# Twelve of 22 inner tiles of two feed-forwards go through the down projection in seven products of halves

## The chip, the cores and the metric

One Trainium2 chip; the kernel uses one of its cores. The metric is the device time of one execution in microseconds (us), measured on the chip. TensorE does the matmuls, VectorE and ScalarE the elementwise work, GpSimd some more of it, and SyncE (SP) issues the transfers between DRAM and the on-chip memory.

## What is computed

Two layers of a transformer trunk over 512 latent tokens and 256 context tokens with 1024 features. Each layer has a feed-forward, a mixer and a second feed-forward, all in float32:

```python
D_MODEL = 1024; SEQ = 512; CTX_LEN = 256; D_FF = 2816
def swiglu(h, w_gu, w_down):
    gu = h @ w_gu
    return (jax.nn.silu(gu[..., :D_FF]) * gu[..., D_FF:]) @ w_down
...
x = x + 0.5 * gt * swiglu(h, p["ffn1_w_gu"], p["ffn1_w_down"])
xc = xc + 0.5 * gtc * swiglu(hc, p["ffn1_w_gu"], p["ffn1_w_down"])
```

`h` is the normalized input, scaled and shifted by vectors of its own for latent and for context tokens; `gt` and `gtc` are gates, one per feature. All these vectors come from a projection of the conditioning (`w_mod`), nine of 1024 features per layer.

## The kernel before

Everything is kept transposed: 128 features on the partitions, 768 tokens in the free dimension, context first. The residual `xs` stays in four on-chip slots `xp` (two feature tiles each); `xd` is a DRAM tensor of the same shape, in which the mixers park the residual. Each float32 matrix is split into an upper part (rounded to TensorE's float32 format, by ScalarE) and a lower part (what is left, by VectorE); a product is the sum of three matmuls, upper-upper, upper-lower and lower-upper. `split` (L125 to L128) does it, for weights as for activations; `load_split` loads and splits a weight.

The stages run in the order first feed-forward, attention pair, second feed-forward, third feed-forward, linear attention, fourth feed-forward. A feed-forward (`ffn`) goes over the inner dimension in 22 tiles of 128. They are grouped in `PARTS` of 6, 6, 5 and 5 tiles. For each tile, gate and up are computed, multiplied and split into `hid[f]` (six buffers). After each part its tiles go through the down projection: for each quarter u of the output (two feature tiles of 128) the weights are loaded, `pair` issues the matmuls for 256 context and 512 latent columns, and `add_gated` (L398) adds the gated result to the residual. The last part goes through `close_out`, which also prepares the next stage's input.

From tile 4 on (5 in the last feed-forward), gate and up are computed by `seven_open`'s `unit`: the matrix [gate; up] times [first half | second half of the tokens] is a 2x2 block product, which is done in seven block products in place of eight (Strassen's method in Winograd's form). The sums of the activations (T1 to T4) are made once per feed-forward, those of the weights (S1 to S4) in each unit, and the sums of the products behind the matmuls, on VectorE and ScalarE. One product is 12 matmuls with 384 columns. The `product` helper accumulates in one bank of a ring of eight.

The conditioning's projection is background work of VectorE: `mod_step` takes steps from a queue, each of which loads 256 KB and does two multiply-and-sum instructions of 512 columns (L297), one for each of the two conditioning vectors. `bg` says how many steps follow each unit and each quarter; `mod_step(1000)` does the rest.

Instructions are written in program order; a scheduler with a model of the engines orders them for each engine before the run. Buffers are rings of fixed size: `raw` three, `whi` and `wlo` three, `sg` one.

Of the kernel before, what the change touches and what calls it, by code (L numbers as in the profile page):

```python
# [21 lines left out]
CTX = 256  # L22
# [3 lines left out]
PARTS = [(0, 6), (6, 6), (12, 5), (17, 5)]  # L26
EPS = 1e-6
# [20 lines left out]
class Net:  # L48
# [54 lines left out]
    def load_split(self, src, n, pool=None, keep=4, slots=(None, None)):  # L103
# [3 lines left out]
        for j in range(2):  # L107
            raw = self.raw(src[:, j * (n // 2):(j + 1) * (n // 2)])
# [10 lines left out]
    def raw(self, src):  # L119
        n = src.shape[-1]  # L120
        raw = self.stage.tile([128, 1024], F32, tag="raw", name="raw", bufs=3)[:, :n]
        self.nc.sync.dma_start(out=raw, in_=src)
        return raw

# [47 lines left out]
    def mod_finish(self, l, p):  # L172
# [4 lines left out]
        for v in range(2):  # L177
# [4 lines left out]
        if p % 3 == 2 and p != 5:  # L182
            nc.vector.tensor_scalar(out=m, in0=m, scalar1=0.5, scalar2=None, op0=ALU.mult)

# [93 lines left out]
    def mod_step(self, n):  # L278
        nc = self.nc
        self.owed += n  # L280
        while self.owed >= 1 and self.pending:
            self.owed -= 1
            l, p, m, i = self.pending.pop(0)
            if i == 0 and m == 0 and p == 0:
                nc.sync.dma_start(out=self.bmod[l], in_=self.ins[f"b_mod{l}"])
                nc.sync.dma_start(out=self.ng[l], in_=self.ins[f"norm_g{l}"])
# [7 lines left out]
            for v in range(2):  # L294
# [4 lines left out]
            if i and m == KT - 1:  # L299
                nc.vector.tensor_tensor(out=self.mod[l][p], in0=self.mod[l][p], in1=self.acc, op=ALU.add)  # L300
                self.mod_finish(l, p)
# [150 lines left out]
    def ffn(self, l, sub, idx, segs, nxt, bg=(0, 0), first=4, start=False):  # L452
# [12 lines left out]
        st = ExitStack()  # L465
        with st:
# [6 lines left out]

            def up(f, ss, regs=None):
# [4 lines left out]
                if f not in hid:  # L479
                    hidden(f)  # L480
                sg = pool.tile([128, T], F32, tag="sg", name="sg", bufs=1)
# [4 lines left out]
                self.split(sg[:, a:b], hid[f][0][:, a:b], hid[f][1][:, a:b])  # L486
# [32 lines left out]
            for pi, (f0, nf) in enumerate(PARTS):  # L519
                for f in range(f0, f0 + nf):  # L520
                    if f >= early:
                        if f >= first:
                            if f == first:
                                sp = seven_start()
                                if self.pending:
                                    self.mod_open(self.pool("modp", sts, side="right"))
                            hidden(f)
                            sg = pool.tile([128, T], F32, tag="sg", name="sg", bufs=1)
                            seven(sp, gu[f], sg, hid[f])
# [6 lines left out]
                dn = self.ins[f"dn{l}{idx}_{nf}"][pi % 2 if nf == 6 else pi - 2]  # L536
                load = lambda u: self.load_split(dn[u], 2 * nf * 128)
                if pi == len(PARTS) - 1:
# [3 lines left out]
                    h = self.close_out(load, nf, xk, segs, gate, nxt)  # L542
                else:
                    for u in range(4):
# [4 lines left out]
                        self.mod_step(bg[1])  # L549
        yield h  # L550

    def seven_open(self, st, h, n0):
# [7 lines left out]
        sub = lambda o, a, b: nc.vector.tensor_tensor(out=o, in0=a, in1=b, op=ALU.subtract)  # L560

# [26 lines left out]
        def weights(a):  # L588
            hi = self.stage.tile([128, 1024], F32R, tag="whi", name="whi", bufs=3)
            lo = self.stage.tile([128, 1024], F32R, tag="wlo", name="wlo", bufs=3)  # L590
            res = []
            for i, x in enumerate(a):
                c = slice(i * 512, (i + 1) * 512)
                self.split(x(), hi[:, c], lo[:, c])
                res.append((hi[:, c], lo[:, c]))
            return res

        def product(o, w, x, first, last):
            for k in range(H):
                y = [a[:, k * 128:(k + 1) * 128] for a in w]  # L600
                for i, (wi, xi) in enumerate(((0, 0), (0, 1), (1, 0))):
                    nc.tensor.matmul(out=o, lhsT=y[wi], rhs=x[k][xi], start=first and k == 0 and i == 0,  # L602
# [1228 lines left out]
```

## Time and profile before

| what | value |
|---|---|
| time, median of 3 runs | 2709.84 us (2709.37 to 2710.6) |
| time of the profiled execution | 2708.46 us |
| its span, first to last instruction | 2706.7 us |
| mean granted clock of TensorE | 0.99 of full speed |
| TensorE busy | 2617.1 us (97%) |
| VectorE busy | 2161.1 us (80%) |
| ScalarE busy | 1196.9 us (44%) |
| GpSimd busy | 171.6 us (6%) |

The profile shows one execution; outside its span lie 1.8 us. Busy times are unions of the instructions' times. Those of matmuls overlap in the records, so the pace of matmuls is read from stretches divided by counts, not from the mean of one. Idle time of an engine that is not the bottleneck costs nothing.

### The profile page before, as it was taken

The page shows a single profiled execution, that of the slowest core. Times are in us where ns is not written, and L with a number is a line of the kernel's source. Part 1 is how long each engine was busy: PE and PEld are TensorE (multiplying, and loading weights), DVE is VectorE, ACT ScalarE, POOL GpSimd, SP SyncE. Part 2 cuts the span into 40 slices and gives each one's busy share as a digit, 9 for nine tenths or more (in the row PEclk, how much of TensorE's full clock was granted, in tenths as well). Part 3 has the DMA queues.
Part 4 walks back from the last instruction along what each step waited for, and adds up shares of the span by engine and source line. Part 5 has one row for each costly group of instructions (what it writes and reads, how often), then busy time and mean ns, then how long its engine had stood idle before and what let it go on. Part 6 is the DMA issues. An engine that isn't in the chain of part 4 may idle for free. (4 is left out here: it accounts for less than half of the span.)

```text
span 2706.7 us, 44030 instructions
## 1 busy us (share of the span) xinstructions
PE 2617.1 (97%) x16800; PEld 2435.1 (90%) x16800; DVE 2161.1 (80%) x4503; ACT 1196.9 (44%) x2254; POOL 171.6 (6%) x206
## 2 busy tenths in 40 slices
PE   7999999999878899999999999999999999999999
PEld 5899999989777789899999999999998998989899
DVE  6789798977888867797988878888777677778677
ACT  4324242445757744242424542424345565435344
POOL 0000000013443200000000000000000121000000
PEclk9999999999989999999999999999999999999999
DMA  8143444431000140433343314343232121422334
GB/s 313 42 150 115 139 132 145 124 126 42 24 24 1 47 141 30 129 114 127 117 141 100 115 63 138 108 145 104 92 116 86 56 71 63 148 71 92 102 106 128
DMA packets 103572, 279.31 MB, mean 103 GB/s; under 512 B 12256, under 2 KB 15200, under 8 KB 101824
## 3 DMA queue, kind: packets, MB, share of 16 engines
q1 hardware_dynamic: 103360, 276.50, 31.4%
q8 instruction: 132, 2.16, 0.3%
q14 instruction: 80, 0.66, 0.1%
HBM read 269.11 MB, written 7.34 MB: 102 GB/s over the span
## 5 line engine op out<-in xcount | busy, mean ns | idle before, releaser
L127 ACT ACTIVATE whi<-raw 128x512 fp32r<-128x512 f32 (+3 forms) x466 | 355.7, 767 | 739.9 <-PE r L374 326.4
L128 DVE TENSOR_TENSOR wlo<-raw,whi 128x512 fp32r<-128x512 f32 (+3 forms) x466 | 399.2, 859 | 81.0 <-ACT whi L127 78.2
L602 PE MATMUL r<-t,whi 128*128 128x384 f32 (+1 forms) x1704 | 400.9, 323 | 1.8 <-DVE u L639 1.3
L602 PE MATMUL r<-hh,wlo 128*128 128x384 f32 (+1 forms) x1136 | 366.1, 323 | 0.0
L602 PE MATMUL r<-hh,whi 128*128 128x384 f32 (+1 forms) x1136 | 365.8, 322 | 0.0
L602 PE MATMUL r<-hl,whi 128*128 128x384 f32 (+1 forms) x1136 | 365.7, 322 | 0.0
L297 DVE SCALAR_TENSOR_TENSOR junk<-wm,cb 128x512 bf16<-128x512 f32 x480 | 329.1, 686 | 13.4 <-ACT cb L276 8.3
L602 PEld LDWEIGHTS r<-t,whi 128*128 128x128 f32 x1704 | 295.6, 188 | 3.2 <-DVE u L639 2.1
L602 PE MATMUL r<-t,wlo 128*128 128x384 f32 (+1 forms) x852 | 273.3, 323 | 0.0
L374 PE MATMUL r<-dh,whi 128*128 128x512 f32 (+1 forms) x952 | 267.3, 345 | 0.8 <-ACT whi L127 0.8
L374 PE MATMUL r<-dh,wlo 128*128 128x512 f32 (+1 forms) x952 | 266.8, 346 | 0.3 <-DVE wlo L128 0.3
L374 PE MATMUL r<-dl,whi 128*128 128x512 f32 (+1 forms) x952 | 266.8, 344 | 0.0
L127 ACT ACTIVATE whi<-s 128x512 fp32r<-128x512 f32 x284 | 174.6, 625 | 182.4 <-DVE s L624 67.0
L602 PEld LDWEIGHTS r<-hl,whi 128*128 128x128 f32 x1136 | 213.4, 188 | 0.8
L602 PEld LDWEIGHTS r<-hh,wlo 128*128 128x128 f32 x1136 | 213.4, 188 | 0.4 <-DVE wlo L128 0.4
L602 PEld LDWEIGHTS r<-hh,whi 128*128 128x128 f32 x1136 | 213.3, 188 | 0.3
L374 PEld LDWEIGHTS r<-dh,wlo 128*128 128x128 f32 x952 | 178.6, 188 | 24.4 <-DVE wlo L128 1.1
L374 PEld LDWEIGHTS r<-dh,whi 128*128 128x128 f32 x952 | 178.0, 188 | 24.5 <-ACT whi L127 2.7
L374 PEld LDWEIGHTS r<-dl,whi 128*128 128x128 f32 x952 | 178.1, 188 | 23.5
L128 DVE TENSOR_TENSOR wlo<-s,whi 128x512 fp32r<-128x512 f32 x284 | 190.7, 684 | 4.4 <-ACT whi L127 3.7
L398 DVE SCALAR_TENSOR_TENSOR x<-r,mod,x 128x512 f32<-128x512 f32 (+1 forms) x168 | 100.1, 632 | 90.8 <-PE r L374 90.3
L602 PEld LDWEIGHTS r<-t,wlo 128*128 128x128 f32 x852 | 159.9, 188 | 0.1
(417 smaller groups left out, 5845.1 us busy)
## 6 DMA issues: line engine op xcount, KB each, us to landing
raw<-gu SPq DMA_DIRECT2D x176, 512.0 KB, 3.9
wm<-w_mod SPq DMA_DIRECT2D x240, 256.0 KB, 2.9
raw<-dn SPq DMA_DIRECT2D x88, 320.0 KB, 2.9
raw<-dn SPq DMA_DIRECT2D x64, 384.0 KB, 3.1
raw<-w_out SPq DMA_DIRECT2D x28, 512.0 KB, 3.8
m<-w_mod0a SPq DMA_DIRECT2D x12, 1024.0 KB, 10.4
raw<-w_in SPq DMA_DIRECT2D x8, 512.0 KB, 4.8
raw<-w_kq SPq DMA_DIRECT2D x8, 512.0 KB, 3.7
```

What stands on the lines that cost most here:

```text
L127: self.nc.scalar.activation(out=hi, in_=src, func=AF.Copy)
L128: (e or self.nc.vector).tensor_tensor(out=lo, in0=src, in1=hi.bitcast(F32), op=ALU.subtract)
L297: nc.vector.scalar_tensor_tensor(out=junk, in0=w, scalar=1.0, in1=self.cb[:, v, :], op0=ALU.mult, op1=ALU.mult, accum_out=self.acc[:, m, v ...
L374: nc.tensor.matmul(out=outs[s][j], lhsT=w[j][wi][:, k * 128:(k + 1) * 128], rhs=xk[k][xi][:, s0:s1], start=(k == 0 and i == 0), stop=(k == ...
L398: self.nc.vector.scalar_tensor_tensor(out=self.xs[m][:, s0:s1], in0=regs[s][j], scalar=gate[:, m, v:v + 1], in1=self.xs[m][:, s0:s1], op0= ...
L602: nc.tensor.matmul(out=o, lhsT=y[wi], rhs=x[k][xi], start=first and k == 0 and i == 0, stop=last and k == H - 1 and i == 2, skip_group_che ...
```

## The change

In the second and third feed-forward the parts become (0, 4), (4, 4), (8, 4), (12, 4) and (16, 6); the three in the middle are marked `by7`. For these, the down projection of four inner tiles and one quarter of the output is a 2x2 block product too: output tiles j = 0, 1, pairs of inner tiles, halves of the tokens (384 columns). It is done in seven products of 2 x 3 matmuls. The results are not summed on chip: ScalarE multiplies each (or a partial sum that accumulates in a bank) by the gate and writes it to a buffer, and GpSimd sends the buffer with an accumulating DMA to `xd`. Before the first such part the residual is written to `xd`; after the last it is read back. Its on-chip slots serve meanwhile as buffers: sums of the hidden tiles, and halves to send.

`finished` makes the sums of the hidden tiles. `unit` is rewritten for all four feed-forwards: weights are split in pieces of 1024 columns, three banks serve in place of four, one accumulates four products and is copied out in between, and a few VectorE operations fall away. In `mod_step` the last four vectors of the second layer are made for one conditioning vector only, and the steps are shared out anew. The weights of a part whose tiles lie in two stored groups are loaded in several pieces.

```diff
+PLAIN = [(f0, n, False) for f0, n in PARTS]
+SEVEN = [(0, 4, False), (4, 4, True), (8, 4, True), (12, 4, True), (16, 6, False)]
...
+    def mod_vectors(self, l, p):
+        return 1 if l == 1 and p >= 5 else 2
...
-            self.owed -= 1
             l, p, m, i = self.pending.pop(0)
+            nv = self.mod_vectors(l, p)
+            self.owed -= nv / 2
...
+            def finished(f, sg):
+                if f not in place:
+                    if f not in hid:
+                        hidden(f)
+                    self.split(sg[:, n0:T], *[x[:, n0:T] for x in hid[f]])
+                    return
+                q = place[f]
+                hidden(f)
+                if q < 2:
+                    sub(sg[:, hi], sg[:, hi], sg[:, lo])
+                    self.split(sg[:, n0:T], *[x[:, n0:T] for x in hid[f]])
+                    return
+                o = self.kept[:, q - 2, :]
+                self.split(sg[:, n0:T], *[x[:, n0:T] for x in hid[f]])
+                sub(o[:, hi], sg[:, hi], o[:, hi])
+                sub(o[:, lo], o[:, hi], o[:, lo])
+                sub(sg[:, lo], sg[:, lo], o[:, hi])
+                hidden(f + 100)
+                self.split(o[:, n0:T], *[x[:, n0:T] for x in hid[f + 100]])
+                self.split(sg[:, lo], *[self.t4[:, i, (q - 2) * n:(q - 1) * n] for i in range(2)])
...
+            def down_seven(sp, f0, u, buf, late):
...
+                raw = self.raw(sum([self.down_weights(l, idx, f0, 4, u, j) for j in range(2)], []))
+                A11, A12, A21, A22 = [raw[:, i:i + 256] for i in range(0, 1024, 256)]
...
+                self.split(raw[:, 0:512], *[x[:, 0:512] for x in w1])
+                nc.vector.tensor_tensor(out=S1, in0=A21, in1=A22, op=ALU.add)
+                sub(S2, S1, A11)
+                self.split(s[:, 0:512], *[x[:, 512:1024] for x in w1])
+                sub(A21, A11, A21)
+                self.split(raw[:, 512:1024], *[x[:, 0:512] for x in w2])
+                sub(A12, A12, S2)
+                self.split(A12, *cut(w2, 2))
...
+                def out(o, x, j, s):
+                    c = sorted({s.start, s.stop, min(max(CTX, s.start), s.stop)})
+                    for a, b in zip(c, c[1:]):
+                        nc.scalar.activation(out=o[:, a - s.start:b - s.start], in_=x[:, a - s.start:b - s.start],
+                                             func=AF.Copy, scale=gate[:, 2 * u + j, int(a < CTX):int(a < CTX) + 1])
+                def send(o, j, s):
+                    d = self.xd[:, 2 * u:2 * u + 2, s] if j is None else self.xd[:, 2 * u + j, s]
+                    nc.gpsimd.dma_start(out=d, in_=o, accum_op=ALU.add)
+                a, b, c = [self.bank()[:, 0:n] for _ in range(3)]
+                product = self.product
+                product(b, wA11, B11, True, True)
+                out(one[:, 0], b, 0, lo)
+                send(one[:, 0], 0, lo)
+                late()
+                product(a, wA12, B21, True, True)
+                out(two[u % 2], a, 0, lo)
+                send(two[u % 2], 0, lo)
+                product(b, wS2, T2, False, True)
+                out(g1[u % 2][:, 0], b, 0, hi)
+                product(c, wS1, T1, True, True)
+                out(g2[u % 2][:, 1], c, 1, hi)
+                product(b, wS3, T3, False, True)
+                out(g1[u % 2][:, 1], b, 1, hi)
+                send(g1[u % 2], None, hi)
+                product(c, wS4, B22, False, True)
+                out(g2[u % 2][:, 0], c, 0, hi)
+                product(b, wA22, T4, False, True)
+                out(one[:, 1], b, 1, lo)
+                send(one[:, 1], 1, lo)
+                return lambda: send(g2[u % 2], None, hi)
...
+                if by7 and not parts[pi - 1][2]:
+                    self.x_move(self.xd, True, [(n0, T)])
+                    self.t4 = self.x_slot(0, [128, 2, T], F32R)
+                    self.kept = self.x_slot(1, [128, 2, T])
+                    halves = [self.x_slot(i, [128, 2, T]) for i in (2, 3)]
...
+                elif by7:
+                    one = sp.tile([128, 2, n], F32, tag="v", name="v", bufs=1)
+                    sg = pool.tile([128, T], F32, tag="sg", name="sg", bufs=1)
+                    two = [sg[:, i * n:(i + 1) * n] for i in range(2)]
+                    late = lambda: None
+                    for u in range(4):
+                        late = down_seven(sp, f0, u, (*halves, two, one), late)
+                        self.mod_step(bg[1])
+                    late()
+                    if not parts[pi + 1][2]:
+                        self.x_new()
+                        self.x_move(self.xd, False, [(n0, T)])
...
+            s = sp.tile([128, 1024], F32, tag="s", name="s", bufs=1)
+            S1, S2 = s[:, 0:512], s[:, 512:1024]
+            wA11, wA12 = weights(raw[0])
+            add(S1, A21, A22)
+            sub(S2, S1, A11)
+            wS1, wS2 = weights(s)
+            sub(A21, A11, A21)
+            wS3, wA22 = weights(raw[1])
+            sub(A12, A12, S2)
+            wS4, = weights(A12)
+            a, b, c = [self.bank()[:, 0:n] for _ in range(3)]
...
+            product(b, wA11, B11, True, True)
+            copy(v[:, 0], b)
+            product(a, wA12, B21, True, True)
+            add(g1, a, v[:, 0])
+            nc.scalar.activation(out=g1, in_=g1, func=AF.Silu)
+            product(b, wS2, T2, False, True)
+            copy(v[:, 1], b)
             product(c, wS1, T1, True, True)
+            copy(v[:, 0], c)
+            product(b, wS3, T3, False, True)
+            copy(u3, b)
+            add(u3, u3, v[:, 0])
             product(c, wS4, B22, False, True)
+            add(g2, c, v[:, 1])
             nc.scalar.activation(out=g2, in_=g2, func=AF.Silu)
+            product(b, wA22, T4, False, True)
+            mult = lambda o, x, y: nc.vector.tensor_tensor(out=o, in0=x, in1=y, op=ALU.mult)
+            mult(g2, g2, u3)
+            mult(g1, b, g1)
+            done()
...
-                "ffn2_0": ffn(0, 2, 2, ALL_SEGS, (1.6, 4.4)), "ffn1_1": ffn(1, 0, 1, ALL_SEGS, (1.6, 4.4)),
+                "ffn2_0": ffn(0, 2, 2, ALL_SEGS, (1, 2, 6), 4, False, SEVEN),
+                "ffn1_1": ffn(1, 0, 1, ALL_SEGS, (1, 2, 6), 4, False, SEVEN),
...
-                n.mod_queue(*{"ffn1_0": [(0, p) for p in range(3, 9)], "ffn2_0": [(1, p) for p in range(5)],
-                              "ffn1_1": [(1, p) for p in range(5, 9)]}.get(s, ()))
+                n.mod_queue(*{"ffn1_0": [(0, p) for p in range(3, 9)], "ffn2_0": [(1, p) for p in range(4)],
+                              "ffn1_1": [(1, p) for p in range(4, 9)]}.get(s, ()))
```

## Rows read from the trace of the kernel before

**Rows 1.** Page: engines' busy time, and clock and transfers in 40 equal slices.

```profile
PE 2617.1 (97%) x16800; PEld 2435.1 (90%) x16800; DVE 2161.1 (80%) x4503; ACT 1196.9 (44%) x2254; POOL 171.6 (6%) x206
...
PEclk9999999999989999999999999999999999999999
DMA  8143444431000140433343314343232121422334
GB/s 313 42 150 115 139 132 145 124 126 42 24 24 1 47 141 30 129 114 127 117 141 100 115 63 138 108 145 104 92 116 86 56 71 63 148 71 92 102 106 128
```

**Rows 2.** Stretches: length, busy of PE, PEld, DVE, ACT, POOL; clock, DMA share, GB/s.

```profile
1104.70:1155.00 50.30, 50.30 (x291) 44.08 (x290) 39.90 (x91) 8.47 (x12) 0.00 (x0) 1.00 0.43 137
1155.00:1242.20 87.20, 87.20 (x505) 87.20 (x505) 77.59 (x150) 37.69 (x69) 0.00 (x0) 1.00 0.34 112
...
449.10:522.30 73.20, 73.16 (x422) 72.84 (x421) 71.79 (x162) 31.76 (x58) 0.00 (x0) 1.00 0.42 134
```

**Rows 3.** The same stretches, matmuls of `pair` alone, then of `product` alone.

```profile
1104.70:1155.00 50.30, 50.28 (x288) 1.00 0.43 137
...
1155.00:1242.20 87.20, 87.20 (x504) 87.02 (x503) 1.00 0.34 112
```

**Rows 4.** Waits of TensorE, 1060 to 2060 us: total, times, longest.

```profile
PE b L362 <- ACT hh L349: 1.1, 1, 1.1
...
PE b L374 <- DVE dl L128: 1.0, 2, 0.5
PE b L374 <- ACT dh L127: 0.7, 2, 0.4
```

**Rows 5.** Groups by shape: busy us, mean ns; 1155-1242 us, then whole span.

```profile
L297 DVE SCALAR_TENSOR_TENSOR junk<-wm,cb 128x512 bf16<-128x512 f32 x24 | 16.4, 684 | 0.0
L128 DVE TENSOR_TENSOR wlo<-raw,whi 128x512 fp32r<-128x512 f32 x17 | 11.6, 685 | 0.2 <-ACT whi L127 0.2
L127 ACT ACTIVATE whi<-raw 128x512 fp32r<-128x512 f32 x17 | 10.7, 630 | 27.6 <-PE r L602 19.4 <-PE r L374 5.1 <-issue 3.1
L639 DVE TENSOR_TENSOR v<-r,v 128x384 f32<-128x384 f32 x11 | 6.1, 554 | 1.8 <-PE r L602 1.8
L128 DVE TENSOR_TENSOR dl<-sg,dh 128x768 fp32r<-128x768 f32 x5 | 4.8, 959 | 1.9 <-ACT dh L127 1.9
L127 ACT ACTIVATE dh<-sg 128x768 fp32r<-128x768 f32 x5 | 4.2, 846 | 5.6 <-DVE sg L658 5.6
L643 ACT ACTIVATE v<-r 128x384 f32<-128x384 f32 x6 | 2.9, 480 | 0.0
...
L128 DVE TENSOR_TENSOR wlo<-raw,whi 128x1024 fp32r<-128x1024 f32 x93 | 114.2, 1234 | 31.6 <-ACT whi L127 30.8
...
L318 DVE TENSOR_TENSOR ss<-ss,sq 128x256 f32<-128x256 f32 x98 | 40.0, 437 | 1.3 <-ACT sq L316 0.5
L316 ACT ACTIVATE sq<-x 128x256 f32<-128x256 f32 x98 | 37.1, 411 | 24.6 <-DVE x L398 12.4 <-DVE ss L318 12.0
```

**Rows 6.** Timeline (start us, length us), end of the second feed-forward's last unit.

```profile
1482.90 0.84 ACT L127 ACTIVATE dh<-sg 128x768 fp32r<-128x768 f32 x1 [1.82 <-DVE sg L658]
1483.78 0.96 DVE L128 TENSOR_TENSOR dl<-sg,dh 128x768 fp32r<-128x768 f32 x1 [0.97 <-ACT dh L127]
...
1483.80 0.51 PE L374 MATMUL b<-dh,whi 128*128 128x256 f32 x2 [0.36 <-ACT dh L127]
1484.79 0.39 PE L374 MATMUL b<-dl,whi 128*128 128x256 f32 x1 [0.49 <-DVE dl L128]
```

**Rows 7.** Transfers: queue; KB and us to landing; SP's issue ns, min/median/max.

```profile
q1 hardware_dynamic: 103360, 276.50, 31.4%
...
y_t<-x SPq DMA_DIRECT2D x8, 256.0 KB, 2.9
xd<-x SPq DMA_DIRECT2D x4, 768.0 KB, 3.8
...
L122 SPq DMA_DIRECT2D raw<-gu x176: 327/328/1408, 5.4 to 2656.9; - x176
```

More of the change, by code (lines that the diff above doesn't have):

```diff
@@ L299, in mod_step @@
             if i and m == KT - 1:
-                nc.vector.tensor_tensor(out=self.mod[l][p], in0=self.mod[l][p], in1=self.acc, op=ALU.add)
+                a, b = [x[:, :, 0:nv] for x in (self.mod[l][p], self.acc)]
+                nc.vector.tensor_tensor(out=a, in0=a, in1=b, op=ALU.add)
                 self.mod_finish(l, p)
@@ L465, in ffn @@
         st = ExitStack()
+        n0 = segs[0][0]
         with st:
@@ L472, in hidden, with new_sg @@
                           pool.tile([128, T], F32R, tag="dl", name="dl", bufs=6))
+            place = {f0 + q: q for f0, nf, by7 in parts if by7 for q in range(nf)}
+            n = (T - n0) // 2
+            lo, hi = slice(n0, n0 + n), slice(n0 + n, T)
+            sub = lambda o, a, b: nc.vector.tensor_tensor(out=o, in0=a, in1=b, op=ALU.subtract)
+            def new_sg(f):
+                if place.get(f, 2) < 2:
+                    return self.kept[:, place[f], :]
+                return pool.tile([128, T], F32, tag="sg", name="sg", bufs=1)
@@ L485, in up @@
                 a, b = ss[0][0], ss[-1][1]
-                self.split(sg[:, a:b], hid[f][0][:, a:b], hid[f][1][:, a:b])
+                if (a, b) == (n0, T):
+                    finished(f, sg)
+                else:
+                    if f not in hid:
+                        hidden(f)
+                    self.split(sg[:, a:b], hid[f][0][:, a:b], hid[f][1][:, a:b])
             main = [(0, CTX), (CTX, T)] if segs[0][0] == 0 else [(CTX, T)]
@@ L548, in ffn, with product @@
                         self.add_gated(regs, u, main, gate)
-                        self.mod_step(bg[1])
+                        self.mod_step(bg[2] if len(bg) > 2 else bg[1])
         yield h
+    def product(self, o, w, x, first, last):
+        for k in range(len(x)):
+            y = [a[:, k * 128:(k + 1) * 128] for a in w]
+            for i, (wi, xi) in enumerate(((0, 0), (0, 1), (1, 0))):
+                self.nc.tensor.matmul(out=o, lhsT=y[wi], rhs=x[k][xi], start=first and k == 0 and i == 0,
+                                      stop=last and k == len(x) - 1 and i == 2, skip_group_check=not first)
     def seven_open(self, st, h, n0):
@@ L560, in seven_open @@
         sub = lambda o, a, b: nc.vector.tensor_tensor(out=o, in0=a, in1=b, op=ALU.subtract)
+        add = lambda o, a, b: nc.vector.tensor_tensor(out=o, in0=a, in1=b, op=ALU.add)
         s2 = ExitStack()
@@ L586, in seven_open, with weights @@
         T1, T4, T2 = [[[a[:, i] for a in x] for x in t_hl] for i in range(3)]
[L588 to L602, printed above, removed]
-                                     stop=last and k == H - 1 and i == 2, skip_group_check=not first)
+        def weights(x):
+            n = x.shape[-1]
+            hi = self.stage.tile([128, 1024], F32R, tag="whi", name="whi", bufs=3)[:, :n]
+            lo = self.stage.tile([128, 1024], F32R, tag="wlo", name="wlo", bufs=3)[:, :n]
+            self.split(x, hi, lo)
+            return [(hi[:, c:c + 512], lo[:, c:c + 512]) for c in range(0, n, 512)]
+        product = self.product
         def start():
@@ L645, in unit @@
[L645 to L651 removed]
+            copy = lambda o, x: nc.scalar.activation(out=o, in_=x, func=AF.Copy)
+            g1, g2 = sg[:, lo], sg[:, hi]
+            product(b, wA11, B11, True, True)
```

98 lines of the change are left out of this document (45 added, 53 removed).

## The prediction

> **What bounds the kernel now.** I read the page first, then the stretches of the second feed-forward (the third has the same shape), then the waits of TensorE, then the costs of single instructions. The page shows TensorE busy for 97% of the span, at a granted clock of nine tenths or more in every slice but one [rows 1], which is the higher of its two levels. Of the engines only VectorE comes near it, with 80%. In the stretches one sees what that means for the place of the change [rows 2]: TensorE is busy for the whole of the 50.3 us of a plain down projection of six tiles and for the whole of the 87.2 us of the six gate-and-up units after it. VectorE is busy 79% and 89% there. From 1060 to 2060 us, which holds both feed-forwards that change, TensorE's longest total of waits on one releaser is 1.1 us [rows 4]. So these stages are bound by TensorE's stream alone. What takes matmuls out of it is worth its full time, as long as nothing else becomes late; and VectorE has about a tenth of its time free to absorb what is added. One stretch of the first feed-forward ran with VectorE at 71.79 of 73.20 us and lost nothing on TensorE [rows 2]: a nearly full VectorE can be hidden, where nothing near waits for it.
>
> **TensorE's saving.** A plain down projection of six tiles is 288 matmuls, half with 256 and half with 512 columns, in 50.28 us [rows 3]: 0.1746 us each at a mean of 384 columns. A unit's 84 matmuls with 384 columns come from 504 in 87.20 us [rows 3]: 0.1730 us each. A quarter of the output (two output tiles, one u of the loop) over four inner tiles costs 4 x 2 x 3 x 2 = 48 matmuls in the plain way, 8.38 us. In seven products of halves it is 7 x 2 x 3 = 42 of 384 columns, 7.27 us. That is 1.11 us saved. Three parts of four quarters in two feed-forwards are 24 quarters: **-26.7 us**. The 10 tiles that stay plain cost what they did. The last part has six tiles in place of five, and its extra tile is one that the middle parts no longer do.
>
> **What VectorE has to do.** In a unit the edit of `unit` takes out little: the weight splits go in pieces of 1024 (1.23 us, against 2 x 0.685), and the output needs five operations of 384 (0.55 each, 2.8 us) in place of five of 384 and one of 768 (0.95) [rows 5]. Splits 4.4, four sums of 512 at 0.69 make 2.7, output 2.8, hidden split 0.96: 10.9 us, some 1.3 less than now. A unit of a seven-product part then adds a subtraction (0.55) for the first two tiles, and three subtractions, a split of 768 and one of 384 (3.2 us) for the last two: 1.9 on the mean. One background step (two at 0.68, each with a short read-out) is 1.5 by estimate. Sum 14.3 us against the unit's 14.53 on TensorE. A quarter has splits of 512, 512, 512 and 256, four sums of 256 (0.44 by the nearest form): 4.2 us, and two steps 3.0: 7.2 against 7.27. The `add_gated` of the plain way falls away. So VectorE is at 98 to 99% through three parts in a row: just under, like the stretch at 71.79 of 73.20. That fits, and costs nothing by its total. What is left is the order: who waits for VectorE at once.
>
> **Into a seven-product part.** Today the last hidden tile is wanted last. At the end of the second feed-forward's last unit the hidden tile's upper part is there at 1483.74 us, the lower at 1484.74, and even behind the matmuls of four other tiles TensorE waits 0.36 and 0.49 us [rows 6]. In the new order the second product wants that tile after 1.04 + 0.52 us, and the third wants the second derived tile. By the durations of [rows 5]: multiply 0.55, upper part 0.85, lower 0.96, with hand-overs 2.75 us; then two subtractions, upper and lower part, 5.75 us. TensorE has the first product, half of the second, and the S1 product to put there, 2.6 us in all; with the next quarter's first products, if their weights are ready, 4.7. The wait is between 0.5 and 3 us, six times; zero only if the next quarter's weights never compete for VectorE, which is 98% full. I take 1.5: **+9 us**, ends 0 and +19.
>
> **Inside a quarter.** Accumulating b over four products means that ScalarE must copy the bank out while one product of 1.04 us runs. A copy of 384 is 0.48 us, a split piece of 512 is 0.63 [rows 5], so a copy that comes just behind a split is out after 1.1 us and a hand-over: about 0.2 late. The copies of the low half are two instructions (the boundary at 256): by 0.41 for 256 and less for 128, some 0.7. ScalarE's sum for a quarter is 3 x 0.7 + 4 x 0.48 + 3 x 0.63 + 0.4 = 6.3 of 7.27 us. The ends are 0 and the whole saving of 1.11 per quarter (26.7 us). I take 0.2 per quarter, one late copy: **+5 us**.
>
> **The sends.** All DMAs of the program go through one hardware queue now, issued from SP [rows 7]; none accumulates, so the price is bounded. A quarter sends seven pieces of 196.6 KB, 1.38 MB, and loads 0.52 MB of weights and 0.52 of background. Moved at what the stretches move per DMA share (137 GB/s at 0.43 [rows 2] is 319 GB/s) this takes 7.6 us; at the first slice of the page (313 GB/s at eight tenths [rows 1], 390) 6.2. That is with an accumulating byte at the price of a plain one. At twice the price it is 11.9 and 9.7. A store of 256 KB lands in 2.9 us [rows 7]. Two of the five sends go to one place (the first and the second product's), so I expect that the second waits on GpSimd's queue for the first to land, and the two sends behind it wait as well; the postponed one goes into that gap. With SP's usual 0.33 us for an issue [rows 7] that chain is 2.9 + 3 x 0.33 = 3.9 us per quarter, with SP's longest of 1.41 it is 1.4 + 2.9 + 3 x 1.4 = 8.5 against 7.27. The nearest row is a plain store, so I take the single price and one u of lag, which the doubled buffers absorb; for the copies that catch on a buffer still being sent, 0.2 per quarter: **+5 us**, ends 0 and +100 (4.6 per quarter less what the units after it drain).
>
> The Trainium skill ("Collectives: The Full Stack", section "The bandwidth ceiling: the fold count and why AG ≠ RS ≠ AR") says that an add in a transfer is slower not for the add but because it needs two reads on the same read ring, which halves the rate. By it the sends would go at the double price, and a quarter would take at least 9.7 us, 1.3 longer than now, which is the fourth case below. No row here shows an accumulating transfer, so the trace neither agrees nor disagrees.
>
> **Moves that I cost at nothing.** The residual goes out to DRAM and back once per feed-forward, 4 x 768 KB each way (3.8 us to land [rows 7]); the first unit's output wants its slot 4.1 us after it starts, and the return has six units, 87 us, before `close_out` reads it. If SP's queue stood behind the last send, the next unit's weights would be late by a landing, 3 us, twice. The background steps that move to other places, and the 64 that use one vector instead of two, are VectorE work under cover of TensorE.
>
> **The other gain.** The shorter output chain (no 768-wide multiply, 0.95 us) and one more tile of cover take away the wait at `close_out`, 0.85 us [rows 6] and as much in the third feed-forward (1.0 and 0.7 us for two of each [rows 4]); counted for all four: **-3 us**, ends 0 and -6.
>
> **Sum.** -26.7 + 9 + 5 + 5 - 3 = -10.7 us on the profiled 2708.46, that is 2697.8. The median shown is 1.4 us above that execution, so I forecast **2699 us** for the median.
>
> **The cases.**
> 1. *Part of the saving is kept*: 2699, between 2689 and 2704. For it: TensorE is alone at the limit now, and each added wait is a fraction of a product. Chance 0.42.
> 2. *All is hidden*: -26.7 - 3 makes 2680. For it speaks that the order of matmuls already changes where a tile is late (the matmuls of one tile fill in for another); against it VectorE at 98%. Chance 0.15.
> 3. *Hand-overs eat it*: 1 us per quarter in front of the bank copies, or 4 us per entry; -26.7 + 24 and the like ends at 2710, no change. ScalarE at 6.3 of 7.27 us speaks for it. Chance 0.21.
> 4. *The sends bind, slower than before*: the quarter lasts as long as its transfers. From 8.4 us per quarter on the saving is gone; at 9.7 it costs 1.3 x 24 = 31 us, with the entries 9 and the -3: 2747; with part of the backlog drained under the next units, 2725 to 2747. For it: the single price alone is already 6.2 to 7.6 us of 7.27. Against: a part is only 29 us of sends followed by 58 us of units that move 112 GB/s. Chance 0.22.
>
> A difference under 0.2% (5.4 us) can't be told from none here. Faster 0.57 (cases 1 and 2), the same 0.21, slower 0.22. For 8 in 10 the range goes from 2680 (half of case 2 lies below) to 2727 (the dearer half or so of case 4 lies above).
>
> **What would show it.** In the profile after: 84 matmuls per unit still in 14.5 us; quarters of 42 matmuls in 7.3 to 7.9 us (a mean above 8.4 refutes me, and shows whether ScalarE's copies or a landing end the waits); a gap of one to two us on TensorE in front of the second or third product of a part, released by VectorE's or ScalarE's split of a derived tile; GpSimd's issues following ScalarE within about 4 us. If copies wait for a DMA from `v`, `sg` or the half buffers, case 4 holds.

## The result, and the profile after

The changed kernel takes 2913.93 us (median of 4 runs, 2911.2 to 2920.66) against 2709.7 us: the ratio is 1.0759, with an interval from 1.0746 to 1.0772. It is 204 us slower. I had forecast 2699 us, and 2727 us was the end of my range.

The page of the changed kernel shows where to look (the lines that answer to [rows 1] and [rows 7]; the last is a transfer's size and its median time from issue to landing):

```profile
PE 2647.5 (91%) x16656; PEld 2469.0 (85%) x16656; DVE 2117.8 (73%) x4254; ACT 1366.3 (47%) x2511; POOL 294.1 (10%) x326
...
PEclk9999999999889999898989999899899999999999
DMA  7243434511000415647473145764725121422334
GB/s 292 61 139 115 142 113 139 174 44 32 23 8 1 163 37 175 153 110 156 105 177 106 59 149 182 176 163 105 163 63 157 39 66 66 135 66 97 99 99 129
...
q1 hardware_dynamic: 114304, 289.87, 30.9%
q0 software_dynamic: 23424, 33.04, 7.3%
...
xd<-x POOLq DMA_DIRECT2D x48, 384.0 KB, 8.2
```

No engine is fuller than before except ScalarE and GpSimd; TensorE's share fell from 97% to 91%, and VectorE's from 80% to 73%. TensorE waits: its idle time grew from 89.6 us (2706.7 less 2617.1) to 261.9 (2909.4 less 2647.5), 172 of the 203 us by which the span is longer. The rest, 30 us, is busy time, though 144 matmuls fewer are done. A second queue is there, GpSimd's, with the sends. TensorE's waits from 1060 to 2260 us, which holds both changed feed-forwards (total us, times, longest), where [rows 4] had 1.1 us at most:

```profile
PE r L697 <- ACT v L777: 95.8, 11, 17.2
PE r L697 <- ACT x L562: 35.5, 14, 9.8
PE r L697 <- ACT v L562: 17.8, 7, 3.4
PE r L697 <- ACT whi L145: 6.0, 7, 1.7
```

L562 is ScalarE's gated copy out of a bank in a quarter; L777 is the copy of a partial sum in the unit behind the quarters. Neither is late by its own work. ScalarE's and GpSimd's own waits over the span say what it is:

```profile
ACT v L562 <- DMA xd<-v: 64.5, 19, 10.2
ACT x L562 <- DMA xd<-x: 46.6, 13, 9.9
...
POOL xd L567 <- DMA xd<-x: 74.9, 18, 8.8
```

A copy waits until the last send from its buffer has landed, and a send waits until the one before it to the same place has landed. There are two such pairs in a quarter: the pieces of the first and the second product, for which GpSimd waits 22.1 us in 11 waits, and the two larger sends from the `x` slots, the 74.9 us of the last row. The stretches of the changed kernel, columns as in [rows 2], are about four quarters (181 matmuls, where four quarters have 168, since some of the units' stand among them), the units behind them, the end of the next four quarters with the wait behind it, and the units after that:

```profile
1305.30:1349.60 44.30, 34.87 (x181) 33.27 (x181) 32.91 (x81) 26.62 (x57) 14.84 (x15) 0.92 0.75 158
1349.60:1424.80 75.20, 58.01 (x325) 57.69 (x325) 44.67 (x77) 29.21 (x48) 5.49 (x5) 0.89 0.44 107
...
1476.00:1492.20 16.20, 1.17 (x8) 0.85 (x6) 3.94 (x6) 2.24 (x5) 3.48 (x4) 0.66 1.00 268
1492.20:1576.20 84.00, 84.00 (x469) 84.00 (x470) 58.15 (x92) 40.70 (x62) 0.00 (x0) 0.96 0.28 84
```

In the quarters TensorE is busy 34.87 of 44.30 us, and DMA 75% (43% in a plain projection, [rows 2]). From 1476 to 1492.2 us TensorE does 1.17 us of work while the DMA engines are wholly busy, and the granted clock is 0.66, a mixture of its two levels: the waits cost again in the clock. Right behind the wait in the timeline below, a matmul of 384 columns takes 0.52 us at a granted clock of 0.50 (1375.2 to 1378 us); at 1.00 it takes 0.34. Once the sends are out, the next units run without a gap. The timeline of one wait (ScalarE, GpSimd and TensorE; start us, length us):

```profile
1352.17 0.73 ACT L562 ACTIVATE v<-r,mod 128x256 f32<-128x256 f32 x2 [2.52 <-DMA xd<-v]
...
1365.36 0.73 ACT L562 ACTIVATE v<-r,mod 128x256 f32<-128x256 f32 x2 [8.51 <-DMA xd<-v]
1374.73 0.49 ACT L777 ACTIVATE v<-r 128x384 f32<-128x384 f32 x1 [8.64 <-DMA xd<-v]
...
1356.61 1.42 POOL L567 DMA_DIRECT2D xd<-v  x1
1357.18 2.09 POOL L567 DMA_DIRECT2D xd<-x  x1
1368.10 1.20 POOL L567 DMA_DIRECT2D xd<-x  x1 [8.83 <-DMA xd<-x]
1368.84 1.38 POOL L567 DMA_DIRECT2D xd<-v  x1
...
1375.28 1.01 PE L697 MATMUL r<-t,whi 128*128 128x384 f32 x2 [17.19 <-ACT v L777]
```

Read it backwards. TensorE stands 17.19 us for the unit's first copy to `v`. That copy waits 8.64 us until the send from the same buffer (issued at 1368.84) has landed. Its contents were copied at 1365.36, 8.51 us late, because the send before it from that buffer, issued at 1356.61, had to land first. Between the two, the send at 1368.84 stood in GpSimd's queue behind one from `x`, which waited 8.83 us for its own pair. So there are two landings in a row, through one single buffer that the quarters share with the unit.

### The profile page after: what moved, and what is told of

It is laid out like the page before. It is cut to its first block, busy times and chain, and to the rows that moved or that the text cites. A ratio compares the mean times of both kernels' runs of the same rounds, so it can differ in the third digit from the quotient of the medians.

```text
span 2909.4 us, 44198 instructions
## 1 busy us (share of the span) xinstructions
PE 2647.5 (91%) x16656; PEld 2469.0 (85%) x16656; DVE 2117.8 (73%) x4254; ACT 1366.3 (47%) x2511; POOL 294.1 (10%) x326
## 3 DMA queue, kind: packets, MB, share of 16 engines
q0 software_dynamic: 23424, 33.04, 7.3%
## 5 line engine op out<-in xcount | busy, mean ns | idle before, releaser
L145 ACT ACTIVATE whi<-raw 128x1024 fp32r<-128x1024 f32 (+3 forms) x506 | 429.0, 854 | 579.3 <-PE r L697 214.3
L146 DVE TENSOR_TENSOR wlo<-raw,whi 128x1024 fp32r<-128x1024 f32 (+3 forms) x506 | 489.5, 973 | 225.3 <-ACT whi L145 222.4
L697 PE MATMUL r<-dh,whi 128*128 128x384 f32 x288 | 105.9, 379 | 62.2 <-ACT x L562 33.2
L777 ACT ACTIVATE v<-r 128x384 f32<-128x384 f32 (+1 forms) x213 | 96.7, 456 | 124.4 <-PE r L697 66.5
L145 ACT ACTIVATE whi<-s 128x1024 fp32r<-128x1024 f32 (+1 forms) x95 | 90.4, 951 | 123.6 <-PE r L697 45.0
L567 POOL DMA_DIRECT2D xd<-v x48 | 52.7, 1115 | 876.9 <-ACT v L562 624.3
L399 PE MATMUL r<-dh,wlo 128*128 128x512 f32 (+1 forms) x408 | 125.4, 358 | 0.0
L399 PE MATMUL r<-dl,whi 128*128 128x512 f32 (+1 forms) x408 | 124.9, 356 | 0.0
L399 PE MATMUL r<-dh,whi 128*128 128x512 f32 (+1 forms) x408 | 124.7, 356 | 0.0
L697 PEld LDWEIGHTS r<-dh,whi 128*128 128x128 f32 x288 | 58.8, 206 | 76.1 <-ACT x L562 38.5
```

Of the source, the lines that this page charges most:

```text
L145: self.nc.scalar.activation(out=hi, in_=src, func=AF.Copy)
L146: (e or self.nc.vector).tensor_tensor(out=lo, in0=src, in1=hi.bitcast(F32), op=ALU.subtract)
L399: nc.tensor.matmul(out=outs[s][j], lhsT=w[j][wi][:, k * 128:(k + 1) * 128], rhs=xk[k][xi][:, s0:s1], start=(k == 0 and i == 0), stop=(k == ...
L567: nc.gpsimd.dma_start(out=d, in_=o, accum_op=ALU.add)
L697: self.nc.tensor.matmul(out=o, lhsT=y[wi], rhs=x[k][xi], start=first and k == 0 and i == 0, stop=last and k == len(x) - 1 and i == 2, skip ...
L777: copy = lambda o, x: nc.scalar.activation(out=o, in_=x, func=AF.Copy)
```

## The experiments

The kernel before, run with them on the same chip each time, took 2708.57 to 2709.97 us. The changes below are against the changed kernel, unless another is named.

**The sends left out** (`e1_no_send`), and **sent without adding** (`e2_plain_send`):

```diff
-                    nc.gpsimd.dma_start(out=d, in_=o, accum_op=ALU.add)
+                    pass                                    # e1_no_send
+                    nc.gpsimd.dma_start(out=d, in_=o)       # e2_plain_send
```

> The changed kernel without its accumulating sends (the down projection's products of the three middle parts are computed and copied out, but never added to the residual). Theory A (what costs is the price of an accumulating byte: the q0 row gives 7.3% of 16 engines' 2909.4 us for 23424 packets, 145 ns for each of some 1536 bytes, which fills the DMA engines and makes each landing late): all waits for a landing go, time 2700 to 2735. Theory B (the hand-offs of the bank that accumulates, and a full ScalarE and VectorE, cost the time; the sends are hidden): 2850 to 2900. Theory C (buffers that are too few, with a chain of waits on GpSimd): as A, 2700 to 2735.

> The changed kernel with sends that write in place of accumulating (so the residual gets only the last piece). Same bytes, same issues, same order, same waits. Theory A: a packet at the price of a plain store, half; the waits shrink with the price, 2720 to 2780. Theory C: a landing is still some 3 us and the chain stays, 2790 to 2860. Theory B: 2890 to 2910.

Measured: 2744.56 us, ratio 1.0132 [1.0087, 1.0177], and 2830.16 us, 1.0448 [1.0414, 1.0481]. Without sends the kernel is slower than theories A and C had it (2735 at the most); with plain sends theory C's range holds, and A's (to 2780) doesn't. So the sends cost 169 us, about half for being sent at all (85.6) and half for adding (83.8); the interval of the first run alone is 12 us to either side. In the page of the plain sends the same bytes on GpSimd's queue are

```profile
q0 software_dynamic: 9984, 33.04, 3.0%
...
xd<-x POOLq DMA_DIRECT2D x48, 384.0 KB, 5.3
```

3.0% of 16 engines over 2829.3 us is 1358 us of engine time, 41 us per MB. The accumulating sends take 7.3% over 2909.4 us, 3398 us, 103 per MB: 2.5 times as much, in 23424 packets in place of 9984. They land in 8.2 us in place of 5.3. The number of packets is not the main part of that price: where the adding sends are fewer and larger (`e6_sums`, below), the row is

```profile
q0 software_dynamic: 3456, 18.88, 3.8%
```

and 3.8% over 2799.0 us is 1702 us, still 90 per MB. The Trainium skill ("Collectives: The Full Stack", section "The bandwidth ceiling: the fold count and why AG ≠ RS ≠ AR") has the rule that I quoted in the prediction, half the rate for an add; it says it of the reducing step of a ring of cores, and I carried it over to a send within one core. The trace agrees with its direction, and the measured price is higher here, 2.2 to 2.5 times in place of 2. And even without sends the kernel is 36 us slower than the kernel before (24 to 48 by the interval): something else is wrong as well.

**The rewritten unit alone** (`e3_unit_only`): all parts plain; of the change the unit and the one-vector background steps are left.

```diff
-                "ffn2_0": ffn(0, 2, 2, ALL_SEGS, (1, 2, 6), 4, False, SEVEN),
+                "ffn2_0": ffn(0, 2, 2, ALL_SEGS, (1.6, 4.4)),
```

and the same for `ffn1_1`.

> Only the rewritten unit and the one-vector background steps of the change; all parts plain, background steps as before. The first and fourth feed-forwards, which have nothing else of the change, took 9.3 and 4.1 us longer. If that is the unit's doing, four feed-forwards make it 20 to 35 us slower than before: 2730 to 2745. If it only shows there by chance of the order, 2705 to 2720.

Measured: 2738.04 us, 1.0108 [1.0077, 1.0139]. The unit, for which I had counted a small gain, costs 29 us by itself.

**A second buffer for the single one** (`e4_other_buffer`): the first product's piece goes to the two halves of `v` by turns, the last one's to `u3`. `e8_plain_other_buffer` does the same with plain sends.

```diff
-                out(one[:, 0], b, 0, lo)
+                out(one[0], b, 0, lo)
...
+                    last = sp.tile([128, n], F32, tag="u3", name="u3", bufs=1)
...
-                        late = down_seven(sp, f0, u, (*halves, two, one), late)
+                        late = down_seven(sp, f0, u, (*halves, two, (one[:, u % 2], last)), late)
```

> The changed kernel with the first product's piece in the two halves of the buffer v by turns and the last product's piece in the unit's free buffer u3, so that neither waits for the same quarter's or the last quarter's landing, and the next unit's first copy does not wait for the last send. Theory C: the waits of the units' first copies (99.5 us in 14 waits) fall to some 20, time 2810 to 2850. Theory A: the engines are as full as before, the waits move to other copies, 2870 to 2905.

> Plain sends (no accumulation) with the first product's piece in the halves of v by turns and the last piece in u3. With plain sends alone 2830, without sends 2744.6. If those 85 us are the one buffer and the wait for a landing of some 3 to 5 us: 2745 to 2785. If they are the engines' time for the bytes, the waits move elsewhere: 2805 to 2830.

Measured: 2851.55 us, 1.0527 [1.0486, 1.0568], and 2773.53 us, 1.0237 [1.0207, 1.0267]. The buffer gives back 62 us with adding sends and 57 with plain ones. The first lies just above theory C's range and well below A's, the second in the range of the one buffer. TensorE's wait on the unit's copy, the longest total with plain sends, goes from 64.9 us to 9.5 with the other buffer (waits, 1060 to 2160 us):

```profile
PE r L697 <- ACT v L777: 64.9, 11, 10.4
```

```profile
PE r L698 <- ACT v L778: 9.5, 7, 4.2
```

So of the plain sends' 85.6 us most was one buffer. With adding sends the same wait falls only from 95.8 to 30.3 us, and the adding price stays, 78 us between these two:

```profile
PE r L698 <- ACT v L778: 30.3, 9, 7.6
```

**The change with the unit of before** (`e5_old_unit`): `weights` and `unit` are put back.

> The changed kernel with the unit of before (four banks, pieces of 512, its own output chain); the seven-product down projection and its sends as in the change. If the unit's cost adds to that of the sends as the unit alone showed (2738.0 against 2708.6, 29 us): 2880. If VectorE, with 1.3 us more per unit, is what the parts run into: 2905 or more. If waits of the units hide behind those of the sends: 2895 to 2910.

Measured: 2849.92 us, 1.0519 [1.0488, 1.0549]: 64 us less, below all that I had expected (2880 at the least). In the old unit no product has to wait for the first copy to `v` before the fifth; TensorE's wait on that copy falls from 95.8 to 7.7 us (1060 to 2110 us). Waits on split weights take part of it back: 16.5 us in place of 2.1 on the lower part, 24.6 in place of 6.0 on the upper.

```profile
PE r L697 <- ACT whi L145: 24.6, 20, 3.8
PE r L697 <- DVE wlo L146: 16.5, 13, 3.2
...
PE r L697 <- ACT v L785: 7.7, 3, 3.5
```

**Fewer bytes to send** (`e6_sums`): VectorE sums the seven pieces of a quarter on chip, and one accumulating send of 768 KB goes out per quarter, with background steps (1.4, 1, 6). `e7_sums_old_unit` has the unit of before as well.

```diff
+                out(x[:, 0, lo], b, 0, lo)
...
+                out(v[:, 0], a, 0, lo)
+                add(x[:, 0, lo], v[:, 0])
...
+                nc.gpsimd.dma_start(out=self.xd[:, 2 * u:2 * u + 2, :], in_=x, accum_op=ALU.add)
```

> The changed kernel with the seven pieces of a quarter summed on VectorE (three additions of 384) into one on-chip slot for the whole quarter, and one accumulating send per quarter: 0.79 MB in place of 1.38 in five sends, no two sends of a quarter to one place, no buffer shared with the units waits for a landing (two slots by turns); background steps 1.4 per unit and 1 per quarter to make room. Price and buffers together explain the 165 us between 2909 and the 2744.6 without sends: then 2745 to 2780. If the price alone did, by bytes 57% of 165 stay: 2820 to 2840. If VectorE's room is the limit (1.65 us more per quarter), 2790 and TensorE waits for VectorE.

> The sums on VectorE and one send, with the unit of before as well. If the unit's 29 us come off: 2716 to 2750, still not below 2708 because the quarters without any send were already 6.5 us dearer than the plain ones. If VectorE is the limit: as with the rewritten unit, or more.

Measured: 2803.28 us, 1.0347 [1.0314, 1.0379], and 2784.43 us, 1.0277 [1.0243, 1.0311]. That is 111 us less than the change for 18.88 MB in place of 33.04, and within a quarter no send waits for another to the same place; but a send still takes 8.6 us to land (9.3 in the second), and TensorE still waits 33.7 us in the second one for the copies into its buffers:

```profile
PE r L688 <- ACT x L563: 33.7, 13, 6.9
```

The first lies in none of its three ranges and the second 34 us above its own; bytes, buffers and order change together here, so the 111 us are not divided among them. The second is the fastest whole version of the seven products that I ran, and it is 75 us behind the kernel before.

**No background in the quarters** (`e12_no_steps`): `bg` is (2, 0, 7) in place of (1, 2, 6), to take their loads off the DMA engines.

> The changed kernel with no background step after the seven-product quarters (two after each unit, seven after each plain quarter), so 0.52 MB less to load per quarter and 3 us less on VectorE. If the engines' time for bytes is what makes the landings late, loads and sends of a quarter fall by some 14 to 20%: 2880 to 2895. If waits go by the chain of single landings: 2900 to 2912. If VectorE's load in the quarters held them: below 2870.

Measured: 2909.37 us, 1.0735 [1.0705, 1.0764]; no gain, as for a chain of single landings. The edit reached only a part: from 1305.3 to 1349.6 us there are 8 multiply-and-sum instructions and 4 of their loads, where the change has 18 and 8. The sends land in 7.6 us in place of 8.2, and TensorE's wait for the unit's copy is what it was:

```profile
PE r L697 <- ACT v L777: 95.2, 10, 20.9
```

That loads beside the sends make them late is thus not seen at this amount; without any such load it was not tried.

**Without sends, piece by piece.** `e9_old_unit_no_send` is the change without sends and with the unit of before. `e10_no_mid_copy` also leaves out the four copies that ScalarE makes between products that go on in the same bank:

```diff
-                out(one[:, 0], b, 0, lo)
-                out(g1[u % 2][:, 0], b, 0, hi)
-                out(g2[u % 2][:, 1], c, 1, hi)
-                out(g1[u % 2][:, 1], b, 1, hi)
```

and `e15_early_tiles` lets every product of `e10` read the part's first two tiles, which are there long before:

```diff
-                T4 = [[self.t4[:, i, k * n:(k + 1) * n] for i in range(2)] for k in range(2)]
+                B21 = T3 = T4 = B11
+                B22 = T2 = T1
```

> The changed kernel with the unit of before and without sends (the middle parts' products never reach the residual). Without sends and with the new unit it was 2744.6. If the unit's 29 us come off whole: 2712 to 2720, about the time of before, so that the 26.7 us that TensorE is spared are given back inside the parts even where sending is free. If the rewritten unit is only dear where nothing else waits: 2725 to 2745. If it costs more inside the parts, as 59 us with the sends did: 2685 to 2700.

> The same, and of ScalarE's seven copies per quarter the four that a bank waits for before it accumulates on are left out too (three of b, one of c; their pieces are missing from the result). If the hand-over of the bank inside the quarter is what gives the saving back: 20 to 30 us less than with them. If it is the entry into a part (VectorE's and ScalarE's sums of the last hidden tile): within 6 us of the kernel with them.

> The kernel with the unit of before, no sends and no copies between products (2712), in which all seven products of a quarter read the first two inner tiles of the part only, so that none waits for the part's last tile or for the tiles derived from it; the sums of the tiles are made but not read. Theory: the entry into a part is what is left of the loss; without it the time falls by 15 us or more, to 2687 to 2697 (the full saving would be 2683). Rival: the splits inside a quarter are late; then it stays within 5 us of 2712.

Measured: 2726.09 us (1.0066 [1.0051, 1.0081]), 2712.34 us (1.0013 [1.0004, 1.0022]) and 2692.9 us (0.9942 [0.9927, 0.9957]). So the unit's share here is 18.5 us, that of the bank copies 13.8, and that of the late tiles 19.4. The first hangs on the run without sends and has its 12 us to either side; the second lies between its two ranges (20 to 30, or within 6); the third is in its theory's range. TensorE's waits in `e10` from 1060 to 2110 us show about half of the third:

```profile
PE r L693 <- ACT dh L145: 6.3, 3, 3.3
PE r L693 <- DVE u L779: 5.0, 2, 3.3
PE r L693 <- DVE dl L146: 3.9, 6, 1.3
PE r L693 <- DVE wlo L146: 2.4, 7, 0.6
```

`dh` and `dl` are the split hidden and derived tiles; in `e15` both rows, 10.2 us in nine waits, are gone, while those on `u` and `wlo` stay (4.9 and 2.3 us). The pages of `e10` and `e15` have the other half as busy time of the same matmuls, 12.3 us less, with a mean granted clock of 0.984 and then 0.987:

```profile
PE 2608.4 (96%) x16656; PEld 2443.2 (90%) x16656; DVE 2173.2 (80%) x4538; ACT 1281.9 (47%) x2462; POOL 171.5 (6%) x206
```

```profile
PE 2596.1 (96%) x16656; PEld 2436.4 (90%) x16656; DVE 2171.7 (81%) x4538; ACT 1281.9 (48%) x2462; POOL 172.6 (6%) x206
```

**Why the unit is slow.** Three tries on `e3_unit_only`. `e11_unit_regroup` puts S3 and S4 into one weight buffer and A22 into its own, so that the buffers come free in another order. `e14_half_splits` splits the weights in pieces of 512 again. `e13_unit_own_banks` gives each product a bank of its own, so that none waits for a copy; the sums of products that the shared banks made are left out:

```diff
-            a, b, c = [self.bank()[:, 0:n] for _ in range(3)]
+            b, a, b2, c, b3, c2, b4 = [self.bank()[:, 0:n] for _ in range(7)]
...
-            product(b, wS2, T2, False, True)
-            copy(v[:, 1], b)
+            product(b2, wS2, T2, True, True)
+            copy(v[:, 1], b2)
```

> The rewritten unit alone (all parts plain), with S3 and S4 split into one weight buffer and A22 into its own, so that the third buffer is free after the sixth product and not after the seventh. If the unit's 29 us are weights that come late because a buffer of the ring of three is held to the unit's last product (the waits for ScalarE's split of a weight are 14.0 us of TensorE's there): 2709 to 2722. If they are the copies of the bank between its products: 2732 to 2740.

> The rewritten unit alone, with its weights split in pieces of 512 columns as before, in the same buffers and the same order. Theory A (copies in one bank): a split in front of a copy is 0.63 in place of 1.06 us, so a gap of 1.0 us becomes 0.6 and the time falls by 5 to 10 us, to 2728 to 2733. Rival (the long pieces make the splits late): it falls by 20 or more, to 2718 or less. VectorE has 0.14 us more per pair of pieces, which costs nothing if it isn't the limit.

> The rewritten unit alone (all parts plain), but each of its seven products goes to a bank of its own, so that no product waits until ScalarE has copied a bank out; the partial sums of products are left out. Theory A: the unit's 29 us come from the copies between two products on one bank, which stand on ScalarE behind splits that wait for a weight buffer; without that link the time falls from 2738 to 2709 to 2716. Rival: the splits themselves are late for TensorE (pieces of 1024 columns, buffers); then it stays at 2732 to 2740.

Measured: 2744.85 us (1.0135 [1.012, 1.015]), 2756.46 us (1.018 [1.0165, 1.0196]) and 2710.66 us (1.0009 [0.9999, 1.0018]). The grouping fell as a cause. Shorter pieces made it slower by 18 us, where I had expected a fall under either theory; TensorE's wait on the unit's copies to `v` grew from 4.5 to 10.2 us over the span, and the rest is not settled. With own banks the interval holds 1, so the unit's 29 us are gone: the cost hangs on the link from a copy to the next product on its bank. In `e3` one sees the copies late on ScalarE, and then TensorE without work:

```profile
1170.33 0.53 ACT L783 ACTIVATE sg<-sg 128x384 f32<-128x384 f32 x1 [0.22 <-DVE sg L709]
1173.47 1.06 ACT L145 ACTIVATE whi<-raw 128x1024 fp32r<-128x1024 f32 x1 [2.61 <-PE r L697]
1174.43 0.85 ACT L777 ACTIVATE v<-r 128x384 f32<-128x384 f32 x2
...
1173.22 0.51 PE L697 MATMUL r<-t,wlo 128*128 128x384 f32 x2
1174.58 0.45 PE L697 MATMUL r<-hh,whi 128*128 128x384 f32 x1 [0.85 <-ACT whi L145]
```

A split for the next unit stands in ScalarE's queue ahead of the copies, and waits 2.61 us until TensorE gives a weight buffer free. Behind it two copies start, the first at 1174.43. TensorE's next matmul starts at 1174.58, just behind the end of the split (1174.53) and before the first copy, which takes 0.47 us, is out. So the row is right that the split released it, and by these times this matmul adds to neither of the copied banks; a product that does can't start before 1174.90, because its copy stands behind the same split. Over the span TensorE's waits on upper weights and unit copies are, in `e3` and then with own banks,

```profile
PE r L697 <- ACT whi L145: 14.0, 16, 1.1
PE r L697 <- ACT v L777: 4.5, 5, 2.5
```

```profile
PE r L697 <- ACT whi L145: 2.7, 1, 2.7
```

so with own banks most of the waits on the splits go too, although the splits are the same. I take it that TensorE, with the product on the shared bank held back, comes to those weights too early; the order of its matmuls by product is not shown.

## Why the prediction was wrong, step by step

Taken away in the order above, the pieces make a sum. From 2709 the calculated saving of 26.7 us leads to 2682.2. What is left in the quarters when nothing of the rest is there adds 10.7 (2692.9). The late tiles add 19.4 (2712.3), bank copies in the quarters 13.8 (2726.1), the unit 18.5 (2744.6), plain sends 85.6 (2830.2), and adding in them 83.8 (2913.9). The shares hold for this order: the unit costs 29 us alone, 18.5 without sends (two values that the noise of two runs each doesn't tell apart), and 64 with them, where its first copy waits on the single buffer. The kernels with changed sends (`e2`, `e4` to `e8`) ran twice each; their intervals reach 8 to 11 us to either side.

- **What bounds the kernel now**: right for the kernel before. But that nothing else was near TensorE was read from busy shares, and what came were landings that no busy share shows.
- **The clock**: put at nothing. Every term was priced with TensorE at the higher level, and a wait only at its own length. The page after has 30.4 us more busy time for 144 matmuls fewer, at a granted clock of 0.96 in place of 0.99. With the calculated saving of 26.7 that makes, by estimate, 57 us of the 204 that are not idle time but matmuls that take longer. Without sends the busy time is 2616.3 us, so 31 of the 57 came with the sends. How much of it the clock alone makes is not separated.
- **TensorE's saving** (-26.7): at least 16 us of it is there, by `e15`. The rest is the 10.7 us of quarters without late tiles and copies, where waits on `wlo` and `u` are left; that term isn't split further.
- **Into a seven-product part** (+9, ends 0 and +19): the mechanism was right, and so were the waits, 10.2 us in nine with 3.3 the longest. What the time fell by was 19.4 us, my upper end: the other half is busy time, beside the lower mean clock, which I had not priced.
- **Inside a quarter** (+5, ends 0 and 26.7): the copies measured 13.8 us, between the ends. I had priced a copy as a little late once per quarter, behind a split that runs; that a split which waits holds a copy up for longer is seen in the unit (`e3`), and not shown for the quarters.
- **The sends** (+5, ends 0 and +100): the step that failed. They measured 169 us. That a send waits for the one before it to land, and that a copy waits for its buffer, stood in the text, though for one pair of sends only: GpSimd stood 22.1 us for that pair, and 74.9 for the other, the two from the `x` slots, which go to one place as well. Wrong were the price, taken from the nearest plain store, which landed in 2.9 us where these take 8.2, and the sentence that the doubled buffers absorb it: the first and the last product's pieces had one buffer, a half each, and the next unit used it too. The upper end counted the bytes and not the landings in a row, and so missed as well.
- **The other gain** (-3): wrong in its sign, +18.5 to +29. I had counted VectorE's work in the new unit and not that four of ScalarE's copies now stand between products on one bank (three on b, one on c), each with a single product in between.
- **Moves that I cost at nothing**: about half the background steps beside the sends, taken away, gained nothing (`e12`). The residual's moves weren't measured by themselves, but SP's queue did stand behind the last sends with the moves back (L94), which the text had put at 3 us, twice, if it came: 53.0 us in eight waits, the longest 10.6. What of it reached TensorE is not known.
- **The cases**: the fourth was right in its sign, and its mark came true (copies that wait for a send from `v` and the half buffers). But it let a quarter last as long as its bytes, and the DMA engines were at 75% there: landings in a row set the time. So its 2725 to 2747 us was too low: 42 matmuls took 10.3 us from 1305.3 to 1349.6 (44.30 us for 181), not 9.7, and the waits at the units behind them were not in it.

## What to carry to other kernels

When a result leaves the chip in pieces, follow the life of each buffer: time to copy, wait to issue, landing under load, next user. A chain of such lives through one buffer sets the pace, however small the bytes. Where no trace shows an accumulating transfer, a plain store elsewhere in the kernel is too cheap a guess: here adding took 2.2 to 2.5 times the engine time and landed in 8.2 us in place of 5.3. Price a wait of TensorE with the slower matmuls behind it. And a copy between two products on one bank should be read in its engine's queue order, with what stands ahead of it and may wait.

## What the runs showed of the hardware

- An accumulating send took 103 us of engine time per MB and a plain one 41, for the same 33.04 MB; the accumulating ones were cut into 2.3 times as many packets. In larger packets (18.88 MB in 3456, `e6`) it still took 90.
- In one kernel, adding sends of 192 KB landed in 6.7 and 7.3 us and those of 384 KB in 8.2; in `e6` and `e7` those of 768 KB took 8.6 and 9.3: the time to land went far less than by size. From 1305 to 1425 us the sends took 3.5 us at the least, 7.4 in the median and 10.6 at the most to land.
- GpSimd took 0.86 to 1.2 us to issue an adding send (medians by form) and 0.54 to 0.72 for a plain one (`e8`), SP 0.33 for its own transfers.
- A wait of TensorE costs beyond itself: in the stretch with 1.17 us of work in 16.20 the granted clock was 0.66, and over the whole kernel it was 0.96 in place of 0.99.
